# Another task order, two more weight buffers and one bias buffer in a hybrid decoder layer with a mixture of experts

## The chip, the cores and the metric

The kernel is one launch on one core of one Trainium2 chip. The metric is the device time of the launch in microseconds (us), smaller is better. Engine names are those of the profile: PE is the matrix engine, DVE, ACT and POOL work on tiles of data, SP here only issues DMA transfers.

## What is computed

One layer on 512 tokens of width 1024: a mixer (a gated DeltaNet with four heads and a sliding-window attention, one input and one output projection for both), then a mixture of 32 experts of which every token takes four.

```python
h = _rmsnorm(x, norm1_w) * (1 + scale1) + shift1
x = x + gate1 * _mixer(h, ...)                     # 512 x 1024 -> 512 x 1024
h = _rmsnorm(x, norm2_w) * (1 + scale2) + shift2
x = x + gate2 * _moe(h, ...)

# _moe
top_val, top_idx = lax.top_k(xf @ w_router + b_router, 4)
gates = jax.nn.softmax(top_val, axis=-1)
# for each expert e, over the tokens xb that chose it:
hu = xb @ w_up[e] + b_up[e]                        # 1024 -> 2048
act = min(glu, 7) * sigmoid(1.702 * min(glu, 7)) * (clip(lin, -7, 7) + 1)
y[tokens] += gate * (act @ w_down[e] + b_down[e])  # 1024 -> 1024
```

In the mixer every chunk of 64 tokens needs the inverse of a triangular 64x64 matrix for each head. The weights of the experts are 32 x 12 MiB in float32.

## The kernel before, in words

**Mixer, 0 to about 430 us.** A small list scheduler, `class Flow`, writes the program. Each piece of work is a Python generator (a task); before each step it yields the engine, a cost in us and the buffers that the step takes. The scheduler looks at the steps that could start, and of those whose start by these costs lies within `SLACK` of the earliest it takes the one of the lowest number in the table `PR`. So the costs and `PR` fix the order of instructions on each engine; they do no work on the chip themselves. The in-projection (`project`, whose matmuls are emitted by `mm3`, L317) splits each float32 product in three matmuls of a faster data type (fp32r); one step is one such triple. The matrices of the DeltaNet are inverted by doubling, in two rounds of two heads each: products `ps_X`, `ps_Y`, `ps_XT` (L818) that each need the one before, with a copy on ACT (L1001) or a subtraction on DVE between them. Other matmuls stand between these products: those of `project`, of the attention (L743 to L794) and of the conditioning vector (`late`, L649).

**Routing.** For each tile of 128 tokens `route(i)` gives the four experts of a token and its place in its expert's list, `table` makes a one-hot product of it (L1183 to L1196), and after the last tile `ranks` sorts the experts by their token counts (L1504 to L1526: the sorted numbers are `eri`), and `places` makes the lists of tokens, `gi` (L1537), and the targets of the results, `si` and `sg` (L1544 to L1550). `finish(i)` adds the experts' down biases to the residual (L1373 on DVE, L1377 on POOL) and stores it (L1381).

**Experts, from about 430 us.** They run in the order `ORDER`, sorted by count, so that the sizes are fixed and only the numbers are read at run time. For place q in this order: `rows_of` gathers the tokens (POOL clears `xg`, L1697, and issues an indirect DMA, L1698), `turn` transposes them on PE (L1711), `up_pass` (L1760), `swiglu`, `turn_act` (L1783), `down` (L1797), `put` (L1804, L1805) scatters the sums into the output. Weights come in chunks of 1 MiB (128 x 2048 float32): 8 of `w_up` (L1654) and 4 of `w_down` (L1663) for each expert. `fetch_up(q)` reads the expert's number from `eri` on SP and issues them. A chunk goes into a buffer that `wslot` names; there are 16, which turn: w (8), x (1), r (3), v (2), vy (1), e (1). Expert 0 is the same always, so that its 12 chunks are loaded during the mixer. SP's transfers use eight semaphores in turn, so that at most eight are in flight. `fetch_up(1)` reads its number not from `eri` but from `second`, a copy made on POOL (L1904) that is ordered behind the first gather.

Biases of `w_up` are small transfers (L1640) into one of two tile sets in turn; `then` issues them after `THEN` = 2 chunks of the up weights (6 for q = 1). `spread_bias` (L1720) copies the rows of such a tile to all partitions; it is emitted one expert ahead of its use.

Of the kernel before, what the change touches and what calls it, by code (L numbers as in the profile page):

```python
# [20 lines left out]
P = 128  # L21
D = 1024
T = 512
# [11 lines left out]
THEN, THEN1 = 2, 6  # L35
RINGS = {"w": RING2 - 1, "x": 1, "r": RING, "v": RING3 - 1, "vy": 1, "e": RINGE}
SLACK = 0.1
CONV_END = "V"
PR = {"swa": 1, "conv": 5, "cend": 4, "in": 4, "late": 1, "z": 2, "load": 1, "yS": 7, "fin": 3, "rt": 4, "yT": 3, "rec": 1, "oout": 2}
# [73 lines left out]
class Flow:  # L113
# [4 lines left out]

    def __init__(self, depth):
        self.depth, self.taken, self.back = depth, defaultdict(int), defaultdict(list)  # L120
        self.free, self.done, self.tasks, self.now = defaultdict(float), {}, [], 0.0
# [21 lines left out]
    def start(self, t):  # L143

        at = max(t[2], self.free[t[3][0][0]])
        for tag in t[3][2:]:
            n = self.taken[tag] - self.depth[tag]
            if n >= len(self.back[tag]):
                return None
            if n >= 0:  # L150
                at = max(at, sorted(self.back[tag])[n])
        return at

    def run(self):
        while True:
# [15 lines left out]
            else:  # L171
                first = min(at for at, _ in can)
                at, t = min((c for c in can if c[0] <= first + SLACK), key=lambda c: (c[1][0], c[0], c[1][1]))
                eng, cost = t[3][0][0], t[3][1]
# [4 lines left out]
                t[2] = at if t[3][0] == "D&" else self.now  # L179
                self.step(t)  # L180


@with_exitstack
def layer_kernel(ctx: ExitStack, tc: tile.TileContext, A, out, probe=None):
# [11 lines left out]
    ring = ctx.enter_context(tc.tile_pool(name="ring", reuse_waits="tile", bufs=RING))  # L196
    dram = ctx.enter_context(tc.tile_pool(name="dram", bufs=1, space=DRAM))
# [250 lines left out]
    def tv(n):  # L448
        return 0.09 + 0.001 * n

    def ts(n):
        return 0.17 + 0.00073 * n

    def tg_(n):
        return 0.2 + 0.002 * n
# [184 lines left out]
    def late(r):  # L640

        pa = None
        for k in range(KT):
            yield [("lw", r, k)]
            yield ("P", 0.5) + (("o",) if k == 0 else ())
            if pa is None:
                pa = bank("o", "ps_ada")
            for j in range(4):
                TE.matmul(pa[32 * j:32 * j + 32, :256], lhsT=bc(cact[:, k:k + 1], [P, 32]), rhs=lw[r, k][:, 256 * j:256 * j + 256],  # L649
                          start=(k == 0), stop=False)  # L650
            flow.give("lp")
        yield "P", 0.45
# [79 lines left out]
    def swa_weights(i, kv):  # L732
# [6 lines left out]
        for jj in range(2):  # L739
            yield "P", 0.0034 * w, "s"  # L740
# [18 lines left out]
        for h in range(4):  # L759
            yield "S", ts(w)  # L760
# [15 lines left out]
    def swa_values(i, kv):  # L776
# [3 lines left out]
        for kt in kts:  # L780
# [12 lines left out]
            yield "P", 0.56  # L793
# [32 lines left out]
    def lengths(p):  # L826
# [5 lines left out]
        for z, name in enumerate("kq"):  # L832
            for j in range(2):
# [5 lines left out]
                yield ("P", 0.3) + (("d",) if ps is None else ())  # L839
# [22 lines left out]
    def decay(p):  # L862
# [29 lines left out]
        for z, name in enumerate("kq"):  # L892
# [3 lines left out]
            yield "P", 1.2, "d"  # L896
# [79 lines left out]
    def inverse(p):  # L976
# [67 lines left out]
        for hp in range(2):  # L1044
            yield "P", 1.2, "d"
# [107 lines left out]
    def out_delta(i):  # L1153
        yield [("wod",), ("yS", i), ("oT", 2 * i + 1)]
        for hf in range(2):
# [7 lines left out]
            flow.add(PR["rt"] - 1, out_end(i, hf, a))  # L1163

    def out_end(i, hf, a):
        yield "V", tv(T), "cv"
# [3 lines left out]
        yield "V", tv(T)  # L1170
# [3 lines left out]
        flow.mark("y", i, hf)  # L1174

# [3 lines left out]
    def table(i, s0, pay, sels):  # L1179


        pay = pay.rearrange("p (k c e) -> p k c e", k=TOPK, c=2)
        V.tensor_tensor(pay[:, :, 0], oha[:, i], bc(slots[:, i, 2, :, None], k3), op=OP.mult)  # L1183
        V.tensor_tensor(pay[:, :, 1], oha[:, i], bc(slots[:, i, 1, :, None], k3), op=OP.mult)
        sel = []
        for k2 in range(2):
            sel.append(sels[k2]().rearrange("p (k s) -> p k s", k=2))
# [33 lines left out]
    def second_norm(i, ssb, h2):  # L1221
        for hf in range(2):
            yield [("y", i, hf)]
            yield "S", ts(T), "s"
# [33 lines left out]
    def route(i):  # L1258
# [13 lines left out]
        flow.add(PR["rt"] - 0.2 * i, second_norm(i, ssb, h2))  # L1272
        room = yield from rooms()
        h2T = []
        for hf in range(2):
# [4 lines left out]
            yield "P", 0.45, "s"  # L1280
# [50 lines left out]
        V.tensor_scalar(slots[:, i, 2], si4, -1.0, C("TOKT", i, i + 1), op0=OP.mult, op1=OP.add)  # L1331
        room = yield from rooms()
        yield "V", 1.6
        pay, sum_ = table(i, 0, pay, [lambda: room[0], lambda: room[1]])
# [15 lines left out]
    def finish(i):  # L1350
# [4 lines left out]
        yield "V", 0.3, "sv"  # L1355
# [11 lines left out]
        for hf in range(2):  # L1367
            yield "P", 0.25, "s"
# [16 lines left out]
    def recur():  # L1385
# [5 lines left out]
        for n in range(8):  # L1391
            vn = ml2.tile([P, 2, P], F32, name="vn", bufs=3)
            ch = slice(64 * n, 64 * n + 64)
            if n:
                yield "P", 0.45, "d"
# [15 lines left out]
            if n < 7:  # L1411
                Snew = ml2.tile([P, 4, P], F32, name="Sst")
                yield "P", 0.45, "d", "d"
# [18 lines left out]
    def output(n, vn, Sst):  # L1432
        ml2 = state["ml2"]
        ch = slice(64 * n, 64 * n + 64)
        yield "P", 0.45 + 0.45 * (n > 0), "s", "on"
# [23 lines left out]
        for p in range(2):  # L1459
            yield "S", ts(P)  # L1460
# [23 lines left out]
    ex = ce.tile([P, 3, NE], F32, name="ex")  # L1484
    kr, perm = (ex[:, q] for q in (0, 1))
# [9 lines left out]
    permc = ex[:, 1:3].rearrange("p c e -> p (c e)")  # L1495

    def ranks():
# [9 lines left out]
        yield "V", 0.4  # L1507
# [4 lines left out]
        yield "V", 0.6  # L1512
# [3 lines left out]
        for c in range(2):  # L1516
            V.tensor_scalar(ex[:, 1 + c], C("IOTA", 0, NE), ec[:, 2:3], C("ISC", c, c + 1), op0=OP.is_equal, op1=OP.mult)
# [3 lines left out]
        TE.matmul(pe[:NE, 0:NE], lhsT=bc(C("PIDX")[:NE], [NE, NE]), rhs=perm[:NE], start=True, stop=True)  # L1521
        TE.matmul(pe[:NE, NE:2 * NE], lhsT=bc(ec[:NE, 1:2], [NE, NE]), rhs=perm[:NE], start=True, stop=True)
# [6 lines left out]
    def places():  # L1529

        yield [("perm",)] + [("ten", i) for i in range(NT)]
        yield "P", 0.5, "d"
        pgi = bank("d", "ps_gi")
        for g in range(ngr):
            TE.matmul(pgi[:, NE * g:NE * g + NE], lhsT=ten[:, P * g:P * g + P], rhs=perm, start=True, stop=True)
# [3 lines left out]
        for w, n in pieces:  # L1539
            yield "P", 0.9, "d"  # L1540
            pv = bank("d", "ps_sl")[:, :2 * n * NE].rearrange("p (b c e) -> p b c e", c=2, e=NE)
            for b in range(n):
                for j in range(P // w):
# [457 lines left out]
```

## Time and profile before

| | us |
|---|---|
| median of three runs (1478.5 to 1484.42) | 1483.18 |
| the profiled run | 1480.72 |
| its span in the trace | 1478.9 |
| PE busy | 1381.5 (93%) |
| DVE, POOL, ACT busy | 563.8, 261.1, 237.8 |
| mean DMA rate | 322 GB/s, 476.16 MB |

Times are those of one profiled execution unless said otherwise. Its run was 1.8 us longer than its span and 2.5 us below the median. The number behind a line (L1654) is the line of the kernel before.

### The profile page before, as it was taken

To read this page: it belongs to the slowest core of one execution; us is meant where nothing else is said; L and a number is where in the kernel's file an instruction comes from. 1 tells how busy PE (TensorE), PEld (TensorE's weight loads), DVE (VectorE), ACT (ScalarE), POOL (GpSimd) and SP (SyncE) were. 2 spreads that over 40 slices of the span, in tenths; PEclk is the share of its full clock that TensorE was granted. 3 is DMA by queue.
4 is the path that set the end of the run, shared out by engine and by line. 5 is a ranking of instruction groups with operands and counts; after the bars stand their busy time and mean duration, and the time that the engine had idled before them with its cause. 6 is when DMAs were issued, how large, how long until landed. Compare 5 with 4: busy or idle time off the path is not lost. (4 is left out here: it accounts for less than half of the span.)

```text
span 1478.9 us, 22303 instructions
## 1 busy us (share of the span) xinstructions
PE 1381.5 (93%) x8586; PEld 601.3 (41%) x8586; DVE 563.8 (38%) x1247; ACT 237.8 (16%) x542; POOL 261.1 (18%) x216
## 2 busy tenths in 40 slices
PE   4999999999879999979999999999999999999974
PEld 3766666765443333322333333333333333343311
DVE  6965567566853222212221231223321323232310
ACT  4354354442211000000000000000000000010000
POOL 2213133202331111101011101102110112211110
PEclk9999999999969999999999999999999999999976
DMA  9655300256349999999999999999998999999995
GB/s 302 212 200 204 113 29 30 58 214 277 116 152 407 409 387 402 396 391 412 411 412 400 379 419 394 384 409 393 410 367 349 403 348 404 393 418 415 414 415 229
DMA packets 104980, 476.16 MB, mean 322 GB/s; under 512 B 13992, under 2 KB 39556, under 8 KB 55714
## 3 DMA queue, kind: packets, MB, share of 16 engines
q1 hardware_dynamic: 91842, 453.16, 77.4%
q0 software_dynamic: 11952, 18.75, 5.5%
q10 hardware_dynamic: 1072, 2.70, 0.5%
q8 instruction: 75, 1.23, 0.3%
q14 instruction: 39, 0.32, 0.1%
HBM read 464.14 MB, written 17.22 MB: 325 GB/s over the span
## 5 line engine op out<-in xcount | busy, mean ns | idle before, releaser
L1760 PE MATMUL ps_up<-we,xTe 128*64 128x512 f32 (+1 forms) x3040 | 622.2, 607 | 21.2 <-DMA we<-in_w_up_dram 16.8
L1760 PEld LDWEIGHTS ps_up<-we,xTe 128*64 128x64 f32 (+1 forms) x3040 | 188.5, 132 | 394.2 <-issue 336.8
L1797 PE MATMUL ps_dn<-we,aT 128*64 128x512 f32 (+1 forms) x1848 | 316.0, 534 | 19.7 <-DMA we<-in_w_down_dram 10.9
L1797 PEld LDWEIGHTS ps_dn<-we,aT 128*64 128x64 f32 (+1 forms) x1848 | 103.7, 129 | 232.2 <-issue 187.2
L1805 POOL DMA_INDIRECT out_dram<-yv,si x52 | 81.7, 1571 | 649.7 <-DVE yv L1804 464.9
L1712 DVE COPY xTe<-ps_xTe 128x256 f32<-128x256 f32 (+3 forms) x35 | 17.5, 501 | 307.4 <-PE ps_xTe L1711 307.4
L1785 ACT COPY aT<-ps_aT 128x512 f32<-128x512 f32 (+1 forms) x52 | 26.0, 530 | 512.5 <-PE ps_aT L1783 509.1
L1769 DVE TENSOR_TENSOR hu<-ps_up,bb 128x512 f32<-128x512 f32 (+1 forms) x52 | 32.1, 617 | 198.8 <-PE ps_up L1760 198.8
L1804 DVE SCALAR_TENSOR_TENSOR yv<-ps_dn,sg,g2p 128x512 f32<-128x512 f32 x38 | 28.5, 751 | 188.3 <-PE ps_dn L1797 187.4
L1771 ACT ACTIVATE hu<-hu 128x512 f32<-128x512 f32 (+1 forms) x52 | 29.8, 573 | 269.4 <-DVE hu L1770 269.4
L1697 POOL MEMSET xg<- 64x1024 f32 (+3 forms) x35 | 37.2, 1084 | 186.0 <-PE ps_xTe L1711 185.8
L317 PE MATMUL ps_ch<-hhi,wih 128*128 128x512 f32 x128 | 58.5, 457 | 0.0
L317 PE MATMUL ps_ch<-hl,wih 128*128 128x512 f32 x128 | 50.8, 397 | 0.0
L317 PE MATMUL ps_ch<-hhi,wl 128*128 128x512 f32 x128 | 50.5, 395 | 0.0
L1720 DVE STREAM_SHUFFLE bb<-bias 128x1024 f32<-128x1024 f32 (+1 forms) x44 | 48.8, 1137 | 0.1
L1712 ACT COPY xTe<-ps_xTe 128x256 f32<-128x256 f32 (+3 forms) x35 | 15.1, 433 | 163.4 <-PE ps_xTe L1711 163.4
L1698 POOL DMA_INDIRECT xg<-h2d,gi x35 | 35.7, 1021 | 16.1 <-POOL xg L1697 8.1
L1711 PEld LDWEIGHTS ps_xTe<-cst,xg 64*128 64x128 f32 (+3 forms) x280 | 24.1, 142 | 32.3 <-issue 23.1
L1783 PEld LDWEIGHTS ps_aT<-cst,act 128*128 128x128 f32 x180 | 24.3, 208 | 28.6 <-issue 25.7
L1711 PE MATMUL ps_xTe<-cst,xg 64*128 64x64 f32 (+3 forms) x280 | 30.1, 249 | 5.1 <-DMA xg<-h2d,gi 2.2
L317 PEld LDWEIGHTS ps_ch<-hhi,wih 128*128 128x128 f32 x128 | 24.2, 189 | 23.2 <-issue 18.0
L1142 PE MATMUL ps_y<-wos,oS 128*128 128x512 f32 x64 | 33.3, 613 | 0.0
(392 smaller groups left out, 1389.0 us busy)
## 6 DMA issues: line engine op xcount, KB each, us to landing
we<-in_w_up_dram SPq DMA_DIRECT2D x256, 1024.0 KB
we<-in_w_down_dram SPq DMA_DIRECT2D x128, 1024.0 KB
wa<-in_w_ada_dram SPq DMA_DIRECT2D x16, 512.0 KB
wi<-in_w_in_dram SPq DMA_DIRECT2D x8, 1024.0 KB
wl<-in_w_ada_dram SPq DMA_DIRECT2D x12, 512.0 KB
oS<-in_w_ada_dram SPq DMA_DIRECT2D x10, 512.0 KB
LL<-in_w_ada_dram SPq DMA_DIRECT2D x10, 512.0 KB
wt<-in_w_in_dram SPq DMA_DIRECT2D x4, 776.0 KB
```

What stands on the lines that cost most here:

```text
L317: TE.matmul(acc, lhsT=w[a], rhs=x_[b], start=start and q == 0, stop=stop and q == 2)
L1142: TE.matmul(a, lhsT=oS[:, j, P * i:P * i + P], rhs=wo[j][:, 512 * hf:512 * hf + 512], start=(j == 0), stop=(j == 3))
L1697: G.memset(xg[:rows_], 0.0)
L1698: state["gather"] = G.indirect_dma_start(out=xg[:rows_], out_offset=None, in_=h2d, in_offset=bass.IndirectOffsetOnAxis(ap=gidx(g)[:rows_], ...
L1711: TE.transpose(pt[:, k, :rows_], xg[:rows_, 512 * hf + P * k:512 * hf + P * k + P], ident[:rows_, :rows_])
L1712: state["turned", hf] = (S.copy if hf else V.tensor_copy)(xt_[:, 4 * hf:4 * hf + 4, :rows_], pt[:, :, :rows_])
L1720: V.stream_shuffle(bbs[w].rearrange("p h n -> p (h n)"), b[w], [0] * 32)
L1760: TE.matmul(t[w * j:w * j + w], lhsT=lhsT, rhs=rhs, start=(k == 0), stop=(k == KT - 1))
L1769: V.tensor_tensor(g, pg, bbs[w][:, 0], op=OP.add)
L1771: S.activation(sgm, g, AF.Sigmoid, scale=1.702)
L1797: TE.matmul(py[u][w * j:w * j + w, 0:m], lhsT=aT[u][:, kt % nf, w * (kt // nf):w * (kt // nf) + w], rhs=wd[kt][:, m * j:m * j + m], start= ...
L1805: G.indirect_dma_start(out=outv[u[1]], out_offset=bass.IndirectOffsetOnAxis(ap=sidx, axis=0), in_=yv, in_offset=None, compute_op=OP.add, b ...
```

## The change

Five things change together.

1. **The scheduler.** The costs of all steps are new (in-projection: two triples a step, at 1.40, as kind "Pr"); going from fp32r work to other work on PE, and back, is given a cost (`SWITCH`); `SLACK` is 0; entries of `PR` are new; the conditioning matmuls of `late` go in groups (`LATES`); the table of a tile is a task of its own (`tabled`).
2. **Ranking first.** `ranks` goes ahead of the last tile's table; `second` is gone and `fetch_up(1)` reads `eri`; `si` and `sg` are made in `targets()`, after the first gathers have been issued.
3. **Two more weight buffers**, `ringn` and `ringz` (18 in all). `ringn`'s space is free during the mixer, so it takes the first chunk of expert 1.
4. **Memory for them.** GpSimd's reserve for descriptors is 4096 instead of the default of 16384, and there is one set of bias tiles instead of two. The bias of place q+1 is now loaded after all eight up chunks of q+1, and must wait until `spread_bias(q)` has read the tile. For q = 1, the bias of place 0 stands behind four chunks, and waits for the clearing of the tiles on POOL.
5. **Clearing** of the first gathers' tiles (`early`) moves from POOL to ACT.

```diff
-SLACK = 0.1
+SLACK = 0.0
+LATES = {0: 3, 3: 6, 6: 8}
...
+    SWITCH = {"Pr": 0.37, "P": 0.1}
...
+        if t[3][0][0] == "P" and t[3][0] != self.kind:
+            at += self.SWITCH[t[3][0]]
...
-        for k in range(KT):
+        for k in range(0, KT, 2):
             yield [("win", c0, k // 4)]
-            yield ("P", 0.66) + (("a",) if k == 0 else ())
+            yield ("Pr", 1.40) + (("a",) if k == 0 else ())
...
-            mm3(a, [w[:, P * j:P * j + P] for w in wins[c0, k // 4][k]], hx[k], k == 0, k == KT - 1)
+            for k_ in (k, k + 1):
+                mm3(a, [w[:, P * j:P * j + P] for w in wins[c0, k // 4][k_]], hx[k_], k_ == 0, k_ == KT - 1)
...
-        flow.add(PR["rt"] - 0.1, ranks())
+        flow.add(PR["rank"], ranks())
...
-    LATE[:RING3] = [(ringo, "v")] * (RING3 - 1) + [(ringy, "vy")]
-    bias = [{w: misc.tile([P, 16 * w], F32, name=f"bias{w}{q}") for w in (32, 64)} for q in range(2)]
-    for b in bias:
-        for t in b.values():
-            G.memset(t, 0.0)
+    LATE[:] = [(ringn, "n"), (ringe, "e")] + [(ringo, "v")] * (RING3 - 1) + [(ringy, "vy"), (ringz, "z")]
+    bias = {w: misc.tile([P, 16 * w], F32, name=f"bias{w}") for w in (32, 64)}
+    for t in bias.values():
+        G.memset(t, 0.0)
...
-            G.memset(xg[:rows_], 0.0)
+            if early:
+                S.activation(xg[:rows_], bc(one[:rows_], [rows_, D]), AF.Copy, scale=0.0)
+            else:
+                G.memset(xg[:rows_], 0.0)
...
-        e = nc.sync.value_load(second if q == 1 else eri[0:1, r:r + 1], min_val=0, max_val=NE - 1)
-
-        def then():
-            for p in range(q) if q == 1 else ():
-                load_bias(ORDER[p], NB[ORDER[p]], bias[p % 2])
-            load_bias(e, NB[r], bias[q % 2])
...
+        e = nc.sync.value_load(eri[0:1, r:r + 1], min_val=0, max_val=NE - 1)
...
-        wu = load_up(ws[0], then, THEN if q > 1 else THEN1)
+        wu = load_up(ws[0], (lambda: load_bias(ORDER[0], NB[ORDER[0]], bias)) if q == 1 else None, THEN)
         if q > 1:
+            load_bias(e, NB[r], bias)
             down_of[q - 1] = load_down(state["dn"])
...
-        behind(G.tensor_copy(second, eri[0:1, ORDER[1]:ORDER[1] + 1]), state["gather"])
         ups = {0: ahead[0], 1: fetch_up(1)}
         xs[1] = rows_of(1)
+        targets()
         xT = {0: turn(xs.pop(0))}
...
-        bbs = {0: spread_bias(NB[ORDER[0]], bias[0])}
+        bbs = {0: spread_bias(NB[ORDER[0]], bias)}
+        load_bias(state["e1"], NB[ORDER[1]], bias)
...
-    nc = bacc.Bacc("TRN2", target_bir_lowering=False, num_devices=1)
+    nc = bacc.Bacc("TRN2", target_bir_lowering=False, num_devices=1, dynamic_dma_scratch_size=4096)
```

**PE, in the first round of inverses.** Here `LL` and `wl` are weights of the conditioning vector, `hhi`, `wih` and their partners those of the in-projection. Before:

```order
L818 MATMUL ps_X<-Y,XT 64x64 x16
L649 MATMUL ps_ada<-LL,cact 32x256 x4
L317 MATMUL ps_ch<-hhi,wih 128x512
L317 MATMUL ps_ch<-hl,wih 128x512
L317 MATMUL ps_ch<-hhi,wl 128x512
L649 MATMUL ps_ada<-wl,cact 32x256 x4
L317 MATMUL ps_ch<-hhi,wih 128x512
L317 MATMUL ps_ch<-hl,wih 128x512
L317 MATMUL ps_ch<-hhi,wl 128x512
L649 MATMUL ps_ada<-wl,cact 32x256 x4
L818 MATMUL ps_Y<-X,BT 64x64 x16
```

Now:

```order
L838 MATMUL ps_X<-Y,XT 64x64 x16
L670 MATMUL ps_ada<-LL,cact 32x256 x8
L674 MATMUL ps_ada<-bada,cst 32x256 x4
L333 MATMUL ps_ch<-hhi,wih 128x512
L333 MATMUL ps_ch<-hl,wih 128x512
L333 MATMUL ps_ch<-hhi,wl 128x512
L333 MATMUL ps_ch<-hhi,wih 128x512
L333 MATMUL ps_ch<-hl,wih 128x512
L333 MATMUL ps_ch<-hhi,wl 128x512
L838 MATMUL ps_Y<-X,BT 64x64 x16
```

Two triples that stood apart between `ps_X` and `ps_Y` now stand together. Over the whole program the 128 triples stand in 76 groups before and in 38 now.

**PE, in the second round of inverses, now.** `ps_l`, `ps_p` and `ps_o` are the attention's.

```order
L838 MATMUL ps_Y<-X,BT 64x64 x16
L814 MATMUL ps_o<-pT,sw 64x512
L838 MATMUL ps_XT<-XT,Y 64x64 x16
L807 MATMUL ps_p<-cst,LL 128x128 x4
L838 MATMUL ps_X<-Y,XT 64x64 x16
L814 MATMUL ps_o<-pT,sw 64x512
L763 MATMUL ps_l<-kS,qS 128x256 x2
L838 MATMUL ps_Y<-X,BT 64x64 x16
L763 MATMUL ps_l<-kS,qS 128x256 x2
L838 MATMUL ps_XT<-XT,Y 64x64 x16
L838 MATMUL ps_X<-Y,XT 64x64 x16
```

Between two of these products stands one short group of the attention or none; before, it was often nine matmuls of the in-projection.

**POOL, where the experts begin.** `y` is the residual with the down biases. Before:

```order
L1377 TENSOR_TENSOR y_3138<-y_3138,bt 128x512
L1381 DMA out_dram<-y_3138 128x512
L1697 MEMSET xg 128x1024
L1697 MEMSET xg 64x1024
L1698 DMA xg<-h2d,gi 128x1024
L1904 COPY second<-eri 1x1
L1698 DMA xg<-h2d,gi 64x1024
L1697 MEMSET xg 96x1024
L1698 DMA xg<-h2d,gi 96x1024
```

Now:

```order
L1402 TENSOR_TENSOR y_3035<-y_3035,bt 128x512
L1406 DMA out_dram<-y_3035 128x512
L1402 TENSOR_TENSOR y_3042<-y_3042,bt 128x512
L1406 DMA out_dram<-y_3042 128x512
L1730 MEMSET xg 96x1024
L1731 DMA xg<-h2d,gi 128x1024
L1731 DMA xg<-h2d,gi 64x1024
L1731 DMA xg<-h2d,gi 96x1024
L1730 MEMSET xg 64x1024
L1731 DMA xg<-h2d,gi 64x1024
L1717 MEMSET bias_4037 128x512
L1717 MEMSET bias_4038 128x1024
```

The last two additions before the gather wait for DVE multiplications that stand behind `gi` on DVE; both additions, both stores and one clearing stand ahead of the first gather now. The clearing of the bias tiles stays behind the fourth gather, and the `MEMSET` ahead of that one clears a tile that PE's first transposes have read.

**SP, where the experts begin, now.** `ISA` rows set up a transfer's address.

```order
L1920 TENSOR_LOAD eri
L1920 ISA x2
L1685 ISA
L1685 DMA we<-in_w_up_dram 128x2048
L1685 ISA
L1685 DMA we<-in_w_up_dram 128x2048
L1685 ISA
L1685 DMA we<-in_w_up_dram 128x2048
L1685 ISA
L1685 DMA we<-in_w_up_dram 128x2048
L1787 UNCONDITIONAL_BRANCH
L1671 DMA bias_4038<-in_b_up_dram 2x2x512 x2
```

Before, six chunks stood ahead of the first bias transfer, and the read was of `second`.

## Rows read from the trace of the kernel before

**Rows 1.** Busy time by stretch; the first line names the columns, (x) counts instructions.

```profile
core 0: us, PE busy (x) PEld busy (x) DVE busy (x) ACT busy (x) POOL busy (x), PEclk, DMA share, GB/s
75.00:410.00 335.00, 324.91 (x2827) 206.07 (x2826) 215.85 (x504) 131.17 (x319) 81.32 (x60) 0.99 0.40 140
434.00:720.00 286.00, 268.55 (x1380) 91.62 (x1382) 69.94 (x126) 20.90 (x38) 41.78 (x38) 0.98 1.02 398
720.00:1130.00 410.00, 406.14 (x2288) 142.10 (x2286) 109.25 (x220) 27.78 (x54) 60.54 (x49) 1.00 1.01 398
1130.00:1205.00 75.00, 75.00 (x433) 26.57 (x431) 22.06 (x47) 5.45 (x10) 6.46 (x6) 1.00 0.90 351
1205.00:1463.00 258.00, 236.98 (x1272) 82.30 (x1268) 68.10 (x151) 18.11 (x38) 38.78 (x30) 0.94 1.01 407
```

**Rows 2.** SP's waits, 1130 to 1205 us: total us, times, longest.

```profile
SPq L1654 <- PE ps_up L1760: 19.5, 7, 7.7
SPq L1654 <- PE ps_dn L1797: 18.6, 5, 7.4
```

**Rows 3.** PE's timeline, a lone triple and the ends of nine matmuls.

```profile
237.17 0.50 PE L317 MATMUL ps_ch<-hhi,wih 128*128 128x512 f32 x1
...
238.05 1.15 PE L818 MATMUL ps_Y<-X,BT 64*64 64x64 f32 x32
...
258.19 0.50 PE L317 MATMUL ps_ch<-hhi,wih 128*128 128x512 f32 x1
...
260.48 0.73 PE L818 MATMUL ps_Y<-X,BT 64*64 64x64 f32 x17
```

**Rows 4.** The steps between products of the inverse: ACT's copy, by line.

```profile
L1001 ACT COPY Y<-ps_Y x10: 563/586/588, 135.9 to 281.2; 128x512 f32<-128x512 f32 x10
```

**Rows 5.** Timeline of all engines, end of routing to the bias tiles' clearing.

```profile
413.13 0.69 DVE L1373 TENSOR_TENSOR bt<-ps_bd,gm 128x512 f32<-128x512 f32 x1
...
413.98 1.26 POOL L1377 TENSOR_TENSOR y<-y,bt 128x512 f32<-128x512 f32 x1 [7.54 <-DVE rt L1228]
...
415.54 0.56 POOL L1381 DMA_DIRECT2D out_dram<-y  x1 [0.30 <-POOL y L1377]
...
426.75 0.17 ACT L1524 CAST eri<-ps_er 32x32 int32<-32x32 f32 x1 [6.20 <-PE ps_er L1522]
...
427.98 0.28 DVE L1537 TENSOR_SCALAR gi<-ps_gi,cse 128x64 int32<-128x64 f32 x1 [0.82 <-PE ps_gi L1535]
...
429.13 1.10 POOL L1698 DMA_INDIRECT xg<-h2d,gi  x1 [7.12 <-issue]
...
430.23 0.18 POOL L1904 COPY second<-eri 1x1 int32<-1x1 int32 x1
...
433.95 1.97 PE L1711 MATMUL ps_xTe<-cst,xg 128*128 128x128 f32 x8 [2.21 <-DMA xg<-h2d,gi]
...
435.99 0.94 POOL L1697 MEMSET xg<- 64x1024 f32 x1 [1.86 <-PE ps_xTe L1711]
437.20 0.95 POOL L1698 DMA_INDIRECT xg<-h2d,gi  x1 [0.27 <-POOL xg L1697]
438.15 2.79 POOL L1687 MEMSET bias<- 128x512 f32 x4
```

**Rows 6.** SP's timeline, where expert 1's weights start: start, duration, issues.

```profile
431.47 11.94 SPq L1654 DMA_DIRECT2D we<-in_w_up_dram  x6
```

**Rows 7.** Busy time by stretch, from that start on, columns as in the first group.

```profile
431.47:444.60 13.13, 10.76 (x43) 4.48 (x44) 3.07 (x5) 0.58 (x1) 7.05 (x9) 0.72 0.93 294
431.47:449.40 17.93, 15.11 (x67) 6.33 (x68) 3.07 (x5) 0.79 (x2) 7.23 (x10) 0.80 0.95 323
```

**Rows 8.** DMA issues of the gathers: count and median us from issue to landing.

```profile
xg<-h2d,gi POOLq DMA_INDIRECT x35, 8.5
```

**Rows 9.** Timeline around one spreading of a bias.

```profile
1214.09 0.33 SPq L1654 DMA_DIRECT2D we<-in_w_up_dram  x1
...
1214.14 0.76 DVE L1720 STREAM_SHUFFLE bb<-bias 128x512 f32<-128x512 f32 x1
```

More of the change, by code (lines that the diff above doesn't have):

```diff
@@ L117 @@
     LAT = {"P": 0.12, "V": 0.2, "S": 0.2, "G": 0.2, "D": 2.5, "N": 0.0}
+    SWITCH = {"Pr": 0.37, "P": 0.1}
     def __init__(self, depth):
         self.depth, self.taken, self.back = depth, defaultdict(int), defaultdict(list)
[L121 removed]
+        self.free, self.done, self.tasks, self.now, self.kind, self.hold = defaultdict(float), {}, [], 0.0, "Pr", False
     def mark(self, *key):
@@ L173, in run @@
                 at, t = min((c for c in can if c[0] <= first + SLACK), key=lambda c: (c[1][0], c[0], c[1][1]))
-                eng, cost = t[3][0][0], t[3][1]
+                if self.hold:
+                    soon = [c for c in can if c[1][3][0][0] == t[3][0][0] and c[1][0] + 1 <= t[0] and c[0] < at + t[3][1]]
+                    if soon:
+                        at, t = min(soon, key=lambda c: (c[1][0], c[0], c[1][1]))
+                kind, cost = t[3][0], t[3][1]
+                eng = kind[0]
+                if eng == "P":
+                    self.kind = kind
                 for tag in t[3][2:]:
@@ L178, in run @@
                 self.now = at + cost + self.LAT[eng]
-                t[2] = at if t[3][0] == "D&" else self.now
+                t[2] = at if kind == "D&" else self.now
                 self.step(t)
+                if t[3] is not None and isinstance(t[3][0], str) and t[3][0][0] == eng and eng in "VSG":
+                    t[2] = min(t[2], at + cost + 0.04)
 @with_exitstack
@@ L1538, in places @@
         flow.give("d")
[L1539 to L1543, printed above, removed]
-                    TE.matmul(pv[w * j:w * j + w, b].rearrange("p c e -> p (c e)"), lhsT=ten[:, 64 * b:64 * b + w], rhs=permc,
-                              start=True, stop=True)
-            yield "S", 0.2
-            S.copy(sg[w], pv[:, :, 1])
-            yield "V", 0.6
-            for b in range(n):
-                V.tensor_scalar(si[w][:, b], pv[:, b, 0], float(P // w), C("JROW%d" % w, b % 2, b % 2 + 1), op0=OP.mult, op1=OP.add)
-            flow.give("d")
     first.close()
@@ L1608, in layer_kernel, with targets @@
     early.close()
+    def targets():
+        for w, n in pieces:
+            pv = pT_.tile([P, 512], F32, name="ps_sl", tag="t")[:, :2 * n * NE].rearrange("p (b c e) -> p b c e", c=2, e=NE)
+            for b in range(n):
+                for j in range(P // w):
+                    TE.matmul(pv[w * j:w * j + w, b].rearrange("p c e -> p (c e)"), lhsT=ten[:, 64 * b:64 * b + w], rhs=permc,
+                              start=True, stop=True)
+            S.copy(sg[w], pv[:, :, 1])
+            for b in range(n):
+                V.tensor_scalar(si[w][:, b], pv[:, b, 0], float(P // w), jrow[:, w // 64, b % 2:b % 2 + 1], op0=OP.mult, op1=OP.add)
     ringe = ctx.enter_context(tc.tile_pool(name="ringe", bufs=RINGE, reuse_waits="tile"))
```

135 lines of the change are left out of this document (76 added, 59 removed).

## The prediction

> **What bounds the kernel now.** I read the busy times by stretch first, since the share of the whole span mixes stretches with different limits [rows 1]. Four things are to be seen there. From 75 to 410 us the mixer keeps PE busy for 324.91 of 335 us, with the DMA at a share of 0.40: PE bounds, and 10.1 us of PE time stand empty. From 434 to 720 us the DMA share is 1.02 at 398 GB/s, and PE waits for 17.45 us: the weights bound. From 720 to 1205 us PE misses 3.9 us in all, and between 1130 and 1205 it misses none while the DMA share falls to 0.90. From 1205 to 1463 us the DMA is full again (1.01, 407 GB/s) and PE waits for 21 us. What happens in the third stretch is told by SP's waits: between 1130 and 1205 us it waits 19.5 and 18.6 us for PE's matmuls, which still read the buffers that the next chunks want [rows 2]. The transfers had caught up with PE and had no place to go, and the time so lost has to be found again after 1205 us, where the transfers set the end. A share of 0.90 instead of 1.01 over 75 us is 8.2 us of DMA time.
>
> So three places set the end: PE's work in the mixer with the serial chain of routing behind it, the moment at which the stream of weights starts again, and the lack of places between 1130 and 1205 us.
>
> **The order in the mixer.** The same 384 matmuls of the in-projection run before and after, in 76 groups of triples and now in 38. A lone triple that starts at 237.17 holds PE until 238.05, 0.88 us; nine matmuls (three triples) from 258.19 end at 260.48, 2.29 us [rows 3]. With s for a triple and o for a group, s + o = 0.88 and 3s + o = 2.29, so s = 0.705 and o = 0.175 us. 38 groups fewer are worth 38 x 0.175 = 6.7 us on an engine with 97% of its time filled. The bounds are nothing, if the time saved becomes waiting, and 7.9 us (a fifth more, for groups whose other neighbour changes kind as well).
>
> Against it stands the second round of inverses. Its products depend on one another through copies of 0.586 us on ACT [rows 4], and where nine matmuls (2.29 us) stood between two products, there is now one matmul group of the attention, and in places nothing. At about ten steps a part of 0.586 us is uncovered, at most 6 us if no filler covers any. But such matmuls have not gone, they fill 10.1 us that were empty elsewhere, and the added cost of holes is paid once. At the end of the mixer a multiplication of 0.69 us that the routing chain doesn't need stands ahead of its steps on DVE at 413.13 [rows 5]; the new order has it behind `gi`. I take +1 us for all of this, between -4 (half of the empty 10.1 us found) and +4.
>
> **Where the weights start again.** Before, `eri` was complete at 426.92 and `gi` at 428.26, the first gather was issued from 429.13 to 430.23, then came the copy `second`, and then the first chunk, at 431.47 [rows 5, 6]: 3.2 us after `gi` and 4.5 us after `eri`. From there to 444.60 the stream ran at 294 GB/s over 13.13 us, 3.86 MB or 3.7 chunks of 1.049 MB, and to 449.40 at 323 GB/s, 5.8 MB or 5.5 chunks [rows 7].
>
> Now SP reads `eri` itself, so the first chunk goes out without the gather, and the buffer `ringn` is free for it; three more follow when routing has left their space, at about `gi`. Then SP stands at the bias of place 0, which waits for the clearing of the bias tiles on POOL. What stands ahead of that on POOL, counted from the end of `gi`: the multiplication on DVE that the first addition waits for (0.69), two additions of 1.26, two stores of 0.56 with 0.30 ahead of each, one clearing of 0.94, which is 5.9 us; the first gather's issue, 1.10, so 7.0 us (before: 430.23, 2.0 us after `gi`); two more gathers follow it. PE's first transposes began 3.7 us after the first gather's issue had ended, and the clearing that waits for them began 2.0 us later [rows 5]. That gives 7.0 + 3.7 + 2.0 = 12.7, then 0.94 of clearing, 0.27 + 0.95 for the fourth gather, and half of the 2.79 us of bias clearing (one set of two): 16.3 us after `gi`, which on the old clock is 444.6. By then the old kernel had moved 3.7 chunks and the new one has moved its 4 and stands dry, so it is 0.3 chunks (0.8 us) ahead and loses a start of the stream. The old start cost 13.13 x (1 - 294/398) = 3.4 us [rows 7, 1]; I take somewhat over half of it, 1.9 us, since SP then issues without a pause between chunks. That makes +1 us.
>
> That rests on a gather landing as fast as the first one did, on empty engines (3.7 us after its issue). The median gather, among weights, lands 8.5 us after issue [rows 8]. Then the clearing ends 4.8 us later, at 449.4, by when the old kernel had moved 5.5 chunks: 1.5 chunks of 2.63 us, and the start of 1.9, so +5.8 us. Nearest is the quick one, since at most four chunks stand ahead of this gather and they are nearly through by then; I take +2, between -1 (the first chunk's lead is kept) and +7 (a late gather with the whole 3.4 us). PE's own later start, some 5 us, lies in the 17.45 us for which it waits in the stretch anyway [rows 1].
>
> *A rule on this.* Behind a full queue, the gather's landing decides. The Trainium skill ("DMA: Bandwidth & Descriptors", section "Queues, rings and completion order") says that each DMA engine takes turns between the queues that have work for it, a packet at a time, so that a gather would not stand behind whole chunks. By that rule the sum would have +1 here instead of +2; the median of 8.5 us [rows 8] says that among full queues it still costs time.
>
> **Two more places.** While PE bounds and the transfers wait for places, two more hold two more chunks: 2 x 1.049 MB at 398 GB/s = 5.3 us of transfer done ahead, which is less than the 8.2 us that stood idle [rows 1]. From 1205 us on the stream sets the end, and the 21 us in which PE waits there leave room for it to end sooner. So -5.3 us; the bounds are -2 (part of the idle time comes from how the places are given back and not from their number) and -8.2 (all of it). No row prices GpSimd's smaller reserve; its transfers are 35 gathers and 52 scatters, each issued one at a time, and I take 0, between 0 and +2 (0.02 us for each of its transfers' issues).
>
> *A rule on this.* The Trainium skill ("SBUF — State Buffer", section "Summary: rules for kernel authors") estimates transfers from HBM at about 358 GB/s. By that, the two chunks would be worth an estimated 5.9 us. The rows here show 398 and 407 GB/s on this core, and they decide.
>
> **One set of bias tiles.** The bias of place q+1 now waits for `spread_bias(q)`, and behind this wait on SP stand the four chunks of `down(q)`. It costs nothing as long as the spreading is over before SP comes there, or SP's transfers in flight (eight, 8 x 2.63 = 21 us) outlast the wait. Near the end of the tight stretch SP issued the last of an expert's up chunks at 1214.09, and the spreading that it would now wait for ran from 1214.14 to 1214.90 [rows 9]: a wait of 0.8 us under 21 us of cover. I take 0, between 0 and +3.
>
> **Sum.** -6.7 + 1 + 2 - 5.3 + 0 = -9.0 us. The profiled run of 1480.72 becomes 1471.7. The median of the runs is 2.5 us above that run, and the runs spread over 6 us; I say 1472.
>
> **The rivals.**
>
> *The order brings nothing.* The products of the inverses, not PE's filling, set the mixer's time: then the saving of 6.7 us turns into waiting at the copies. For it speak the thinner fillers in the second round; against it speaks that PE was 97% busy, and that the attention's and the in-projection's matmuls have to run anyway. 1480.7 + 1 + 2 - 5.3 = 1478.4.
>
> *More than the sum.* The fitted costs fill half of the empty 10.1 us as well (-5), the restart costs nothing, and the places recover all 8.2 us: 1480.7 - 6.7 - 5 - 8.2 = 1460.8. For it speaks that costs near the real ones let the scheduler see which product will be late.
>
> *The restart goes badly.* The gather lands late, +5.8 instead of +2: 1475.5.
>
> *Slower: the single bias set drains the stream.* If SP's lead over `spread_bias` is short where the DMA bounds, SP stands with an empty queue, and each such stop costs a new start: 3.4 us by the start of before, worked out above. The two DMA-bound stretches hold 286 + 258 us, and an expert's 12 chunks take 31.6 us there, so about 17 experts. To turn -9.0 into +7.4 it takes five of them; eight give 27 us, 1499. It is decided where a wait of SP for DVE passes 21 us. Against it stands [rows 9].
>
> **How the numbers follow.** About 0.5%, 7.4 us, is what a measurement of this kernel can tell from no change: below 1473.3 from the profiled run is faster. The sum has 0.52, with 1466 to 1477 as its own range, and two thirds of that (0.35) below 1473.3; more than the sum 0.20; no gain from the order 0.10; the bad restart 0.08, of which 0.03 faster; the drained stream 0.10. Faster 0.35 + 0.20 + 0.03 = 0.58, within 0.5% 0.32, slower 0.10. The range of 8 in 10 goes from 1459 to 1481: the upper end takes in the order that brings nothing with its bounds, and leaves the drained stream out.
>
> **What would show it.** In the mixer, groups of the in-projection half as many, and PE's busy time from 75 us to the routing some 6 us shorter, with its empty time still near 10 us. The first chunk of expert 1 ahead of `gi`, a pause on SP for POOL's clearing of the bias tiles that ends about 16 us after `gi`, and a DMA share below 1 in that pause. Between 1130 and 1205 us (or where PE then has no waits), a DMA share of nearly 1, and waits of SP for PE that are shorter. No wait of SP for DVE above 2 us. The prediction is wrong if the mixer's end doesn't come sooner, if the pause lasts beyond 20 us, or if the two places are filled and the DMA share there stays at 0.90.

## The result and the profile after

The changed kernel took 1462.11 us (median of four runs, 1461.71 to 1462.85) against 1483.21 for the kernel before: a ratio of 0.9867, with a 95% interval of 0.9847 to 0.9886. It is faster, by 21.1 us; the prediction had said 1472. The two profiled spans are 1459.9 and 1478.9 us, 19.0 apart.

The busy times by stretch of the changed kernel, with the columns of [rows 1]; the first and the last stretch end sooner, since routing and the stream now do:

```profile
75.00:400.00 325.00, 316.69 (x2849) 211.85 (x2847) 214.37 (x510) 133.24 (x325) 76.21 (x57) 0.98 0.40 143
434.00:720.00 286.00, 275.67 (x1482) 93.66 (x1478) 75.89 (x139) 21.27 (x39) 37.63 (x32) 0.99 1.01 405
720.00:1130.00 410.00, 404.77 (x2246) 141.81 (x2246) 108.14 (x215) 29.07 (x56) 59.97 (x49) 1.00 1.01 396
1130.00:1205.00 75.00, 74.36 (x417) 27.09 (x409) 22.16 (x61) 4.17 (x8) 10.17 (x9) 1.00 0.91 354
1205.00:1440.00 235.00, 215.52 (x1154) 72.51 (x1154) 62.07 (x127) 16.67 (x35) 33.60 (x26) 0.96 1.02 409
```

Between 1130 and 1205 us the DMA share is 0.91, where it was 0.90. But PE comes to the same work 15 us sooner now, so the stretch to hold against the old one (0.90, 351 GB/s) is 1115 to 1190 us:

```profile
1115.00:1190.00 75.00, 75.00 (x431) 26.52 (x431) 22.00 (x47) 5.41 (x10) 6.46 (x6) 1.00 0.93 369
```

The two places have filled it in part. What has moved most is where the experts begin. These are rows of the timeline of all engines there in the changed kernel, others between them left out; they answer to [rows 5] and [rows 6]:

```profile
406.82 0.17 ACT L1551 CAST eri<-ps_er 32x32 int32<-32x32 f32 x1 [3.45 <-PE ps_er L1549]
408.05 4.73 SPq L1685 DMA_DIRECT2D we<-in_w_up_dram  x4
411.08 0.28 DVE L1564 TENSOR_SCALAR gi<-ps_gi,cse 128x64 int32<-128x64 f32 x1 [0.78 <-PE ps_gi L1562]
412.51 1.26 POOL L1402 TENSOR_TENSOR y<-y,bt 128x512 f32<-128x512 f32 x1 [1.63 <-DVE bt L1398]
417.93 1.11 POOL L1731 DMA_INDIRECT xg<-h2d,gi  x1 [0.18 <-issue]
425.70 1.94 PE L1744 MATMUL ps_xTe<-cst,xg 128*128 128x128 f32 x8 [9.57 <-DMA xg<-h2d,gi]
427.71 0.94 POOL L1730 MEMSET xg<- 64x1024 f32 x1 [6.08 <-PE ps_xTe L1744]
427.74 0.83 ACTq L1406 DMA_DIRECT2D out_dram<-y  x2
428.92 0.96 POOL L1731 DMA_INDIRECT xg<-h2d,gi  x1 [0.27 <-POOL xg L1730]
429.88 1.43 POOL L1717 MEMSET bias<- 128x512 f32 x2
431.33 1.20 SPq L1671 DMA_DIRECT2D bias<-in_b_up_dram  x2
```

`gi` ends at 411.36 (428.26 before): 16.9 us sooner. The first chunk goes out at 408.05 (431.47): 23.4 us sooner. PE's first transposes begin at 425.70 (433.95): only 8.2 us sooner, since the gather's issue begins 6.6 us after `gi`, and PE starts on its rows 6.7 us after that issue has ended. (Here and below a gather's landing is counted so, from the end of its issue to PE's start on its rows, unless said otherwise.) And SP stands from 412.8 to 431.3 at the bias. The DMA engines are full for the first 11 us of that and not behind it (columns of [rows 1]):

```profile
412.80:424.00 11.20, 3.33 (x37) 1.85 (x35) 3.75 (x12) 2.55 (x5) 7.43 (x8) 0.50 1.02 366
424.00:431.30 7.30, 5.60 (x22) 2.85 (x24) 0.69 (x1) 0.58 (x1) 3.32 (x4) 0.63 0.61 156
```

How the lead goes on is read from the start of PE's transposes for later experts, one row each in its timeline. The first three rows are of the kernel before (experts at places 9, 22 and 31 in the order), the other three of the changed one:

```profile
683.76 0.88 PE L1711 MATMUL ps_xTe<-cst,xg 96*128 96x96 f32 x8
1120.14 0.71 PE L1711 MATMUL ps_xTe<-cst,xg 64*128 64x64 f32 x8
1408.45 0.68 PE L1711 MATMUL ps_xTe<-cst,xg 32*128 32x32 f32 x8
```

```profile
665.50 0.88 PE L1744 MATMUL ps_xTe<-cst,xg 96*128 96x96 f32 x8
1105.08 0.71 PE L1744 MATMUL ps_xTe<-cst,xg 64*128 64x64 f32 x8
1393.31 0.68 PE L1744 MATMUL ps_xTe<-cst,xg 32*128 32x32 f32 x8
```

The lead is 8.2 us at the first transposes, 18.3 at place 9, 15.1 at places 22 and 31, and 19.0 at the end. So it grows up to place 9, where PE had to wait for weights, shrinks by 3.2 us (2.2 of them between places 21 and 22), and grows by 3.9 us behind place 31. Nearly all of this last piece (3.7 us) is one instruction, at the end of the program on POOL (rows by line, ns min/median/max); first before, then after:

```profile
L1997 POOLq DRAIN  x3: 46/109/5378, 1472.7 to 1478.7; - x3
```

```profile
L2032 POOLq DRAIN  x3: 46/109/1662, 1457.4 to 1459.7; - x3
```

### The profile page after: what moved, and what is told of

It reads as the page before. It is cut to its first block, busy times and chain, and to the rows that moved or that the text cites. A ratio compares the mean times of both kernels' runs of the same rounds, so it can differ in the third digit from the quotient of the medians.

```text
span 1459.9 us, 22275 instructions
## 1 busy us (share of the span) xinstructions
PE 1367.2 (94%) x8586; PEld 602.2 (41%) x8586; DVE 558.9 (38%) x1247; ACT 239.5 (16%) x544; POOL 255.8 (18%) x213
## 5 line engine op out<-in xcount | busy, mean ns | idle before, releaser
L333 PE MATMUL ps_ch<-hhi,wih 128*128 128x512 f32 x128 | 55.0, 430 | 0.0
L1745 ACT COPY xTe<-ps_xTe 128x256 f32<-128x256 f32 (+3 forms) x35 | 15.1, 433 | 171.1 <-PE ps_xTe L1744 171.1
```

The source lines that it names most:

```text
L333: TE.matmul(acc, lhsT=w[a], rhs=x_[b], start=start and q == 0, stop=stop and q == 2)
L1745: state["turned", hf] = (S.copy if hf else V.tensor_copy)(xt_[:, 4 * hf:4 * hf + 4, :rows_], pt[:, :, :rows_])
```

## The experiments

All ratios are to the kernel before on the same chip; the changed kernel's is 0.9867. The last three columns are from each trace, in us: when `gi` ends, when the first chunk of the second expert is issued, and when PE's transposes for place 9 begin.

| experiment | ratio | 95% interval | `gi` ends | first chunk | place 9 |
|---|---|---|---|---|---|
| 1 old order, rest new | 0.9958 | 0.9944 to 0.9971 | 429.5 | 429.3 | 683.7 |
| 2 new order, rest old | 0.9989 | 0.9975 to 1.0003 | 413.9 | 423.6 | 677.0 |
| 3 16 places | 0.9890 | 0.9870 to 0.9910 | 412.2 | 412.3 | 668.5 |
| 4 stores sooner | 0.9849 | 0.9825 to 0.9874 | 411.3 | 408.0 | 664.3 |
| 5 as 3, old reserve | 0.9886 | 0.9865 to 0.9907 | 413.9 | 414.0 | 668.7 |
| 6 number copied behind the gather | 0.9967 | 0.9952 to 0.9981 | 409.9 | 418.8 | 672.1 |
| 7 as 4, gather first | 0.9843 | 0.9820 to 0.9866 | 414.1 | 410.8 | 664.5 |
| 8 bias sooner | 0.9923 | 0.9903 to 0.9943 | 414.0 | 410.7 | 671.7 |
| 9 before, reserve 4096 | 0.9972 | 0.9959 to 0.9984 | 429.2 | 432.4 | 683.7 |
| 10 table in route | 0.9886 | 0.9866 to 0.9906 | 416.4 | 413.1 | 673.5 |
| 11 single triples | 0.9992 | 0.9979 to 1.0004 | 429.7 | 426.3 | 685.0 |
| 12 `late` one by one | 0.9924 | 0.9899 to 0.9950 | 418.6 | 414.6 | 672.8 |

**1 and 2: the order alone, the rest alone.** The first has the scheduler, its costs, priorities and steps of before in the changed kernel, and with them the ranking where it stood before; the second has the new order and the new `ranks` with the places, bias sets, reserve, clearing and the copy `second` of before. Two places of the first one's edit:

```diff
-SLACK = 0.0
+SLACK = 0.1
...
-        for k in range(0, KT, 2):
+        for k in range(KT):
```

> Changed kernel with the old scheduler (old costs, slack, priorities, single steps, table inside route), all the rest of the change kept. If the gain lies in the mixer's order (16.9 of 19.0 us by the trace), the lists of tokens are ready near 428 us again and the time is 1478 to 1482. By the prediction's own sizes (order -5.7, places and restart -3.3) it would be 1468 to 1472.

> New order and ranking first, with the old 16 places, two bias sets, the copy of the expert's number on POOL, POOL's clearing and the default reserve. If the order is worth 16.9 us and the rest 2.1, 1463 to 1467; by the prediction's sizes, 1476 to 1479; if the earlier end of the mixer is lost again in the experts without the new places, 1470 or more.

Neither theory held. With the old order the rest is worth 0.4%, and with the old rest the new order is worth nothing that can be told from no change, yet both together give 1.3%. Of the 0.4%, about 0.3 is what the reserve alone gives (experiment 9 below), and at place 9 the first experiment stands where the kernel before does (683.7): without the new order the rest has no other gain that shows. The second experiment's trace says why the order's lead is lost: `gi` ends 14.4 us sooner than before, but the first chunk goes out at 423.65, 7.8 us sooner. The copy `second` stands behind the first gather on POOL, and that behind the additions of the third tile, which the new order has moved behind `gi`. Most of what is left (6.8 us at place 9) is lost between places 21 and 22, where PE waits 4.1 us for weights of `w_down` (1.0 before) and takes 43.8 us instead of 39.0.

**6: the direct read of the expert's number alone.** The changed kernel with `second` again.

```diff
+    second = const.tile([1, 1], I32, name="second")
...
-        e = nc.sync.value_load(eri[0:1, r:r + 1], min_val=0, max_val=NE - 1)
+        e = nc.sync.value_load(second if q == 1 else eri[0:1, r:r + 1], min_val=0, max_val=NE - 1)
...
+        behind(G.tensor_copy(second, eri[0:1, ORDER[1]:ORDER[1] + 1]), state["gather"])
```

> Changed kernel with the first chunks of expert 1 reading a copy of their number that POOL makes behind the first gather, as before the change. If the moment of the first chunk sets the time up to the ninth expert (252 to 257 us from that chunk to the ninth expert's start in six traces), the first chunk moves from 408 to about 419.5 us and the time to 1469 to 1474. If the pause behind the fourth chunk swallows the lead anyway (SP waits until 431 us in both), the time stays at 1462 to 1464.

Rows of its timeline of all engines, others between them left out:

```profile
405.33 0.17 ACT L1551 CAST eri<-ps_er 32x32 int32<-32x32 f32 x1 [3.45 <-PE ps_er L1549]
416.44 1.10 POOL L1731 DMA_INDIRECT xg<-h2d,gi  x1 [0.18 <-issue]
417.55 0.18 POOL L1939 COPY second<-eri 1x1 int32<-1x1 int32 x1
418.79 2.51 SPq L1685 DMA_DIRECT2D we<-in_w_up_dram  x4
```

`eri` was ready at 405.5 and SP started at 418.8. The ratio is 0.0100 over the changed kernel's, 15 us of 1482, more than the 7 to 12 expected: with the new order in place, this one read carries most of the gain. The profiled spans are 14.1 us apart: 6.6 us at place 9, 3.4 more between places 21 and 22, 4.1 elsewhere. The gather, with no weights ahead of it, landed 3.5 us after its issue, and PE's transposes began 4.6 us sooner than in the changed kernel; it helped nothing. PE waited 15.3 us for weights between 600 and 690 us (9.1 in the changed kernel, 11.4 before).

**3: the two places.**

```diff
-    LATE = [(None, "v")] * RING3 + [(ringe, "e")] * RINGE + [(ringn, "n"), (None, "z")]
+    LATE = [(None, "v")] * RING3 + [(ringe, "e")] * RINGE
...
-    LATE[:] = [(ringn, "n"), (ringe, "e")] + [(ringo, "v")] * (RING3 - 1) + [(ringy, "vy"), (ringz, "z")]
+    LATE[:] = [(ringe, "e")] + [(ringo, "v")] * (RING3 - 1) + [(ringy, "vy")]
```

> Changed kernel without the two new places, all else kept; the first chunk then waits for the lists of tokens. If two places are worth what the prediction said (5.3 us, and the first chunk's lead up to 1), 1467 to 1469. Rival: the stall between 1130 and 1205 us comes from how places are given back, and two places are worth under 2 us: 1462 to 1464.

The ratio is 0.0023 higher, 3.4 us, and the intervals overlap. In the trace the loss stands at 3.0 us at place 9, stays 3.0 to place 31 and is 4.9 at the end. So the places count where weights are short before place 9: the first chunk needs a free one at 408, and PE waits 11.2 us there instead of 9.1. In the tight stretch the transfers do fall behind without them; PE comes to its work 3 us later here, and the row that answers to 1115 to 1190 us is

```profile
1118.00:1193.00 75.00, 75.00 (x433) 26.56 (x432) 22.08 (x47) 5.45 (x10) 6.46 (x6) 1.00 0.86 339
```

which is 30 GB/s less over 75 us, 2.25 MB or two chunks. From place 22 to place 24 the share is 0.93 to 0.95 in the eight traces with 18 places and the late bias, and 0.88 to 0.92 in the five with 16. But up to place 31 no time is lost by it, and the last 1.9 us can't be put down to it by this one trace: from place 31 to the end of PE's work the fourteen traces take 57.1 to 60.7 us, and kernels with 18 places are found up to 59.9.

**4 and 7: SP's pause.** The bias tiles are cleared so late in the changed kernel because on POOL their clearing stands behind the fourth gather, and that behind the clearing of a tile that PE's first transposes read (427.71, 428.92 and 429.88 above). The last two stores of the residual are ordered behind the same transposes (427.74); whether they too would hold the tiles' space is not shown, as the clearing starts the moment the fourth gather's issue is over. The fourth experiment drops the order of these stores and clears right behind the first gather; the seventh also takes the third tile's additions and stores off POOL, and has POOL clear the first gathers' tiles again. The fourth's edit:

```diff
-    for t in bias.values():
-        G.memset(t, 0.0)
...
+        for t in bias.values():
+            behind(G.memset(t, 0.0), state["gather"])
...
-        for d in stores[-2:]:
-            behind(d, state["turned", 1])
```

> Changed kernel with the last two stores of the residual no longer ordered behind the first transposes, and the bias tiles cleared right behind the first gather's issue. In the changed kernel SP stands 18.4 us for that clearing. If the pause costs the stream its chunks (about one chunk and a start, 2.5 to 5 us), 1457 to 1460; if it is covered (the stores and gathers fill the DMA meanwhile), 1461 to 1463.

> The fourth experiment's kernel, with the third tile's two additions and stores on DVE and ACT, so that nothing but the clearing stands ahead of the first gather on POOL: PE's first transposes come 6 to 8 us sooner (near 420 us, not 427). If the stream of weights sets the time up to the ninth expert, PE waits those us there and the time is that of the fourth experiment within 2 us (1459 to 1461). If PE's start sets it, 1453 to 1455.

SP's pause at the clearing shrank from 18.4 us to the stretch from 412.7 to 422.1 in the fourth. But two chunks later SP stood again, until PE's first matmuls of the experts (429.08 to 434.54) were through; of SP's waits from 420 to 440 us:

```profile
SPq L1685 <- PEq L1785: 9.5, 1, 9.5
SPq L1671 <- POOL bias L1937: 9.3, 1, 9.3
```

So the half that was taken off the pause came back as a wait for PE, which neither theory had. PE later waited 5.6 us at places 7 and 8 together instead of 7.2. The gain at place 9 is 1.2 us and in the ratio 0.0018, inside the intervals: faster than the changed kernel, but not shown. In the seventh the gather was issued at 415.67, 3.9 us sooner than in the fourth, but with weights in flight it landed 9.5 us after its issue was over, and the transposes began at 426.28 (427.21). So the expected 6 to 8 us at PE didn't come and the run doesn't tell its theories apart. These two have the lowest medians of all, 1460.44 and 1458.78 us.

**8: the single bias set.** The next expert's bias behind four of its chunks.

```diff
-        wu = load_up(ws[0], (lambda: load_bias(ORDER[0], NB[ORDER[0]], bias)) if q == 1 else None, THEN)
+        wu = load_up(ws[0], (lambda: load_bias(ORDER[0], NB[ORDER[0]], bias)) if q == 1 else (lambda: load_bias(e, NB[r], bias)), THEN)
...
-            load_bias(e, NB[r], bias)
```

> Changed kernel with the bias of the next expert loaded behind four of its up chunks instead of all eight. In the changed kernel DVE waits 192.6 us for these loads (31.3 before), and near 1065 us that holds PE's transposes for 2.1 us. If this wait is the price of the single set, it goes and the time is 1459 to 1461, unless SP then waits for the spreading on DVE: then the stream loses 1 us and more at many experts, 1464 to 1475.

In the waits of the changed kernel's DVE (440 to 1450 us) and SP (460 to 1450 us), with us in total, times and longest, the price of the single set has two sides:

```profile
DVE bb L1753 <- DMA bias<-in_b_up_dram: 192.6, 17, 18.9
...
SPq L1671 <- DVE bb L1753: 8.8, 2, 5.7
```

and in this experiment's:

```profile
DVE bb L1753 <- DMA bias<-in_b_up_dram: 69.2, 13, 9.2
...
SPq L1671 <- DVE bb L1753: 47.3, 8, 18.4
```

Sooner is worse, by 0.0056 (8 us): the wait moves from DVE, where it mostly costs nothing, to SP, where the weights stand behind it, and PE waits 5.6 us at place 7 and 6.3 at place 30. The hold of PE's transposes near 1065 us did go (2.1 to 0.3 us).

**5 and 9: GpSimd's reserve.** One argument each: back to the default in the kernel of the third experiment, and to 4096 in the kernel before.

```diff
-    nc = bacc.Bacc("TRN2", target_bir_lowering=False, num_devices=1)
+    nc = bacc.Bacc("TRN2", target_bir_lowering=False, num_devices=1, dynamic_dma_scratch_size=4096)
```

> The kernel with 16 places of the third experiment, with GpSimd's descriptor reserve back at the default of 16384; nothing else differs. In the traces so far POOL's last drain takes 5.38 us in the two kernels with the default and 1.66 us in the four with 4096. If the reserve sets it, the drain is 5.4 us here and the time 3.7 us over the third experiment's ratio to before (0.989): ratio 0.9915. If the drain follows the bias tiles or the places, it stays at 1.7 us and the ratio at 0.989.

> The kernel before, with GpSimd's descriptor reserve at 4096 and nothing else changed. If the reserve sets POOL's last drain, it falls from 5.38 to 1.66 us, and the time by 3.7 us: ratio 0.9975. If the drain is no part of the time that counts, or other work takes its place, the ratio is 1.000 within its interval.

POOL's drain follows the reserve and nothing else that was varied: 5.38 us in the three kernels with the default, 1.58 to 1.66 in the other eleven. In the ninth the time falls with it: 0.9972, 4.2 us. Row of the ninth:

```profile
L1997 POOLq DRAIN  x3: 46/109/1662, 1473.2 to 1475.4; - x3
```

The fifth has the long drain, but its ratio is not above the third's (0.9886 and 0.9890); with half intervals of 0.002 each, 3.7 us (0.0025) can neither be seen nor excluded there.

**10 to 12: parts of the order.** The table back inside `route`; one triple a step; `late` in steps of one.

```diff
-        flow.add(PR["ten"][i], tabled(i, pay, pte, tag))
+        yield from tabled(i, pay, pte, tag)
...
-        if i == 0:
+        if not state.get("tenset"):
+            state["tenset"] = True
```

```diff
-        for k in range(0, KT, 2):
+        for k in range(KT):
...
-            yield ("Pr", 1.40) + (("a",) if k == 0 else ())
+            yield ("Pr", 0.70) + (("a",) if k == 0 else ())
...
-            for k_ in (k, k + 1):
+            for k_ in (k,):
```

```diff
-LATES = {0: 3, 3: 6, 6: 8}
+LATES = {k: k + 1 for k in range(8)}
```

> Changed kernel with each tile's table back inside its route task (its priority and place), all other costs and priorities new. In eight traces the lists of tokens are ready at 409.9 to 414.1 us with the new order, 428.3 and 429.5 with the old; PE waited 7.5 us for the tables' columns before and 0.5 after. If this split gives those 7 us, the lists are ready at 418 to 422 and the ratio is about 0.991. If the costs alone keep PE fed, 410 to 415 and 0.987.

> Changed kernel with the in-projection stepped by one triple at cost 0.70 instead of two at 1.40: its triples stand in 53 groups (38 in the changed kernel, 76 before). By 0.175 us a group the matmuls of the in-projection take 2.6 us more, and their neighbours about 1 more: lists ready at 414 to 418, ratio 0.989. If the number of groups doesn't matter, 410 to 414 and 0.987.

> Changed kernel with the conditioning matmuls in steps of one again, not in groups of three, three and two. Those 288 matmuls took 20.45 us of PE before and 17.57 after. If the grouping gives the 2.9 us, they are back near 20.4, the lists are ready 3 us later and the ratio is 0.989; if not, the time is that of the changed kernel within 1 us (0.9867).

In the eight traces with the new order whole or nearly so (the changed kernel and experiments 2 to 8) `gi` ends between 409.9 and 414.1 us, so differences under 4 us mean nothing here. The tenth's 416.4 is 2 us beyond: its waits for the tables' columns stay at 0.5 us and new ones of 3.0 and 2.6 us come elsewhere, so the 7 us were not that wait. The twelfth moves `gi` to 418.6 with PE's time for `late` at 21.1 us (18.3 in the changed kernel). The eleventh, thought to cost 4 us, takes the whole gain of the order: `gi` at 429.7. Its 53 groups cost the in-projection 3.9 us, and the rest is what PE does meanwhile. Busy time of the out-projection's matmuls (`ps_y`) up to the end of the recurrence of the DeltaNet, and from there to `gi`; before, changed, eleventh:

```profile
75.00:340.60 265.60, 12.75 (x24) 3.75 (x24) 2.08 (x3) 0.99 0.36 119
340.60:428.30 87.70, 50.62 (x104) 17.80 (x104) 8.94 (x13) 0.92 0.48 186
```

```profile
75.00:340.70 265.70, 22.92 (x43) 7.34 (x43) 3.46 (x5) 0.98 0.35 119
340.70:411.40 70.70, 41.07 (x86) 14.78 (x86) 7.57 (x11) 0.93 0.59 230
```

```profile
75.00:340.20 265.20, 12.98 (x25) 3.72 (x25) 1.38 (x2) 0.98 0.36 119
340.20:429.70 89.50, 52.95 (x104) 19.01 (x104) 9.65 (x14) 0.88 0.47 183
```

The recurrence, a serial chain, ends at 340.2 to 340.7 us in all three. PE's time saved ahead of it is not seen as an earlier end there; it holds 19 more matmuls of the out-projection, and these are missing from the queue of work behind it. With one triple a step PE was busy 256.05 us up to that end (262.30 in the changed kernel) and only one was drawn ahead. The tenth and the twelfth lie between: 41 and 35 of these matmuls ahead of the recurrence's end (43 in the changed kernel, 24 before), and `gi` at 416.4 and 418.6.

## Why the prediction was right and where it was wrong

The direction and the range were right: faster, by a change in the mixer's order and in the supply of weights. But the sum was -9.0 us, and the profiled runs lie 19.0 apart: the size was half of what came, and several terms were wrong. The rival *more than the sum* gave 1460.8, close to the profiled run's 1461.71, by other terms than those that came: it has 8.2 us for the places and nothing for the read of `eri` or for the drain. That its number came out is luck.

What the mixer gave shows in the columns of [rows 1] from 75 us to the end of `gi`, before and now:

```profile
75.00:428.30 353.30, 337.22 (x2901) 214.48 (x2901) 230.13 (x552) 134.32 (x331) 86.79 (x66) 0.98 0.39 136
75.00:411.40 336.40, 324.30 (x2890) 217.49 (x2889) 223.97 (x550) 134.22 (x331) 78.66 (x60) 0.97 0.40 142
```

PE is busy 12.9 us less (some 6 had been forecast) and stands empty 4.0 us less (16.1 to 12.1), together the 16.9 us by which `gi` comes sooner.

**The in-projection's groups, -6.7 us.** The mechanism was right, the size too small: PE's busy time for these matmuls fell from 109.8 to 100.6 us, 9.2 us, beyond the bound of 7.9. That is 0.24 us for each of the 38 groups, and 0.26 for each of the 15 of experiment 11, where one pair of rows had given 0.175.

**Holes and routing, +1 us.** The failed step: it took the rest of the mixer as the same matmuls with some waits more. `gi` came 16.9 us sooner (14.1 to 18.4 over the runs of the new order), where the two terms gave 5.7, and 11.9 at their bounds. Behind the recurrence the kernel has 9.5 us less of the out-projection (50.62 to 41.07), 2.9 less of the routing's own matmuls (`ps_rt`, 16.8 to 13.9) and 3.2 less of PE's empty time (11.9 to 8.7). Experiments 10 to 12 take away 5, 18 and 7 us, more than 16.9 in all, so the parts of the order can't be priced one by one.

**The restart, +2 us.** The pause came where it was forecast and by POOL's order. It ended 20.0 us after `gi` (16.3 and 21.1 were the two cases), mostly because the gather landed 6.7 us after its issue and not 3.7. The late case had mixed two counts: the 8.5 us of [rows 8] run from the start of an issue, and so counted the first gather took 4.8, not 3.7. Like for like that case ends 3.7 us behind the quick one, at 20.0. What the pause costs is not shown, since the half that experiment 4 takes off it comes back as a wait for PE. What was priced wrong is the direct read of `eri`, a lead of at most 1 us. Without it the new order's own work behind `gi` stands ahead of the first chunk, and 15 us go (experiment 6).

**Two more places, -5.3 us.** The transfers did what was forecast in part: in the tight stretch the share is 0.93 instead of 0.90 (0.86 in experiment 3), not nearly 1, and SP's two waits for PE from 1115 to 1190 us are not shorter (17.5 and 22.7 us; 19.5 and 18.6 in [rows 2]). But the gain in time (3.4 us, with overlapping intervals) lies elsewhere: 3.0 us up to place 9, none from there to place 31, and 1.9 behind it that one trace can't settle.

**The reserve, 0 us.** Wrong: -4.2 us, in a drain at the very end that the prediction did not look at.

**The single bias set, 0 us.** The waits came: 2.1 us of PE at one expert, by DVE standing at a load. SP too stood at DVE, for up to 5.7 us, where no wait above 2 had been forecast; in the kernel as changed no loss of PE is seen behind that. Experiment 8 made the rival that drains the stream real: SP's longest wait was 18.4 us, and the kernel lost 8 us.

**What bounds the kernel** was read too coarsely. Up to place 9 the stream of weights counts for more than PE's start. In experiment 1 PE started 7.5 us later than before, the first chunk went out 2.2 us sooner, and place 9 came at the same time; in experiment 6 PE started 4.6 us sooner than in the changed kernel, the chunk went out 10.7 us later, and place 9 came 6.6 us later. The spread alone doesn't decide it: from the first chunk to place 9 the fourteen traces take 251 to 261 us, and from PE's start 237 to 251.

What stays open: why the time between places 21 and 22 varies (38.3 to 44.6 us), and whether the versions 4 and 7 beat the changed kernel. And no run takes back the new priorities alone (that of one out-projection task, `yS`, went from 7 to 4.5), or the clearing on ACT alone.

## What to carry to other kernels

Price an early read by what stands in the queue that it skips after the change, not before it: work that a new order pushes behind a result may land ahead of the next transfer. Time saved ahead of a serial chain counts only if later work can be drawn into it, so count the work left behind the chain. Compare a stretch with the one that has the same work, not with the same time on the clock. And read the last instructions of a trace, drains too.

## What was not expected of the hardware

POOL's last drain took 5.38 us with a descriptor reserve of 16384 and 1.58 to 1.66 us with 4096. An indirect gather of 0.5 MB, the experts' first, landed 3.5 to 4.3 us after its issue in the four traces in which no chunk of weights had been issued by then (before, experiments 2, 6 and 9), and 6.5 to 9.6 us after it in the ten in which three or four had.
